# Low parts of the weights by accumulating transfers from memory, in a one-core RWKV-7 / Conformer / gated-MLP layer

## The chip, the cores and the metric

The kernel runs on one core of a Trainium2 chip. A core has five engines that run their own instruction queues in order and wait for one another through semaphores: PE (TensorE, matmuls), DVE (VectorE), ACT (ScalarE), POOL (GpSimd) and SP (SyncE, which here issues the transfers). Sixteen DMA engines move data between the device memory and the core's on-chip memory of 128 partitions. Matmuls write to PSUM, which PE, DVE and ACT reach. The metric is the time of one execution on the device in microseconds (us); lower is better.

## The reference

One layer (DEPTH = 1) on x of 1024 tokens and 1024 channels, in float32: a token mixer made of an RWKV-7 head group and a causal convolution group, then a gated MLP with a short causal convolution. All large products are with weights that come from memory.

```python
h = _rms_norm(x, norm_pre_mix[i])
p = h @ w_in                                  # (1024, 1024) x (1024, 2720)
# RWKV-7 recurrence over 8 heads of 64, causal depthwise conv of width 31, norms, gates
mix = jnp.concatenate([rwkv_out, c], axis=-1) @ w_out        # (1024, 1024) x (1024, 1024)
x = x + _rms_norm(mix, norm_post_mix[i])
h = _rms_norm(x, norm_pre_ffn[i])
hid = h @ ffn_up                              # (1024, 1024) x (1024, 5632)
hid = _causal_dwconv(hid, ffn_conv_w, ffn_conv_b)
gate, up = hid[..., :D_FF], hid[..., D_FF:]   # D_FF = 2816
f = (jax.nn.gelu(gate, approximate=True) * up) @ ffn_down    # (1024, 2816) x (2816, 1024)
x = x + _rms_norm(f, norm_post_ffn[i])
```

## The kernel before

Large products are made of three passes over PE in the type float32r. Each float32 operand is cut into a high part (the value rounded to float32r) and a low part (the value minus the high part), and the product is high x high + high x low + low x high. `split` (L145 to L148) makes the two parts: a cast by ACT, a subtraction by DVE or, with `pool=True`, by POOL.

Weights pass through `weight` (L150 to L160). Per piece of 128 x 512 elements, 256 KB, it takes a raw tile (tag `wr`, three buffers), has SP load it (L154), takes a high and a low tile (tags `wh` and `wl`, two buffers each) and calls `split` on POOL. With `held` the pair comes from another pool and is kept. `weight` is run at high priority, so that its instructions stand in each queue as early as the buffers allow. A buffer is given out again when the last reader of its former content is done; that wait, with the order of the instructions in each engine's queue, sets when a weight's cast can start. The order is fixed when the program is built: a scheduler simulates the program and places instructions by priority, stream by stream (`stream`, `PRIO`).

Who uses weights:

- `project` (called for w_in, w_wa, w_g in the mixer, and for ffn_up by `ffn_pair`): two pieces of a column block of 128 channels; per piece four k tiles x three matmuls of 512 tokens, the third of each three with the low part. The tokens go in two halves of 512, so every weight is loaded twice: 40 pieces of w_in and two each of w_wa and w_g per half, 88 of ffn_up per half.
- `w_out`: 16 pieces per half, 24 matmuls of 256 columns each.
- `ffn_down`: per half 2 x 22 pieces, each with four token tiles x three matmuls, the second with the low part. In the last column half of the last token half, the last eight pieces are `held`.

The mixer runs first (up to about 770 us in the profile), with the recurrence, convolutions and projections interleaved on PE; the first eight channel tiles of ffn_up for the first token half (32 pieces) run inside it. From there on the kernel is ffn_up and ffn_down, first for tokens 0 to 511, then for 512 to 1023. While these run, ACT evacuates each ffn_up bank (L800, `acc<-pb`), then applies gelu (L810) and rounds the result (L148, `ahi`); DVE adds the taps of the short convolution (L805).

Other work on POOL: the power -0.5 of `rstd` (L143), copies and clears, and in the recurrence the scaling of the state (L632, `XG`).

Of the kernel before, what the change touches and what calls it, by code (L numbers as in the profile page):

```python
# [13 lines left out]
F32 = mybir.dt.float32  # L14
F32R = mybir.dt.float32r
BF16 = mybir.dt.bfloat16
AF = mybir.ActivationFunctionType
ALU = mybir.AluOpType
# [73 lines left out]
class Trunk:  # L92
# [57 lines left out]
    def weight(self, src, shape, held=False):  # L150

        with self.tc.high_priority():
            raw = self.wp.tile(shape, F32, tag="wr", bufs=3, name=self.nm("wr"))
            self.nc.sync.dma_start(raw, src)  # L154
            if held:
                hi, lo = (self.hp.tile(shape, F32R, tag="h", name=self.nm("w")) for _ in range(2))
            else:
                hi, lo = (self.wp.tile(shape, F32R, tag=t, bufs=2, name=self.nm(t)) for t in ("wh", "wl"))
            self.split(hi, lo, raw, True)
        return hi, lo  # L160


# [946 lines left out]
```

## Time and profile before

| | us |
|---|---|
| runs shown, three: lowest, median, highest | 1423.25, 1438.39, 1440.5 |
| the profiled execution, its time | 1419.05 |
| the profiled execution, span from first to last instruction | 1417.2 |

The profile's numbers are those of one execution, with a mean granted TensorE clock of 0.978. Busy time is the time in which an engine ran an instruction; waits and the issuing of transfers are not in it. A row of a group gives the line, engine and operation, output <- inputs with buffer numbers left out, shape and count, then busy us and mean ns of one, then the idle time of the engine just before these instructions and what ended most of it. The chain of work that ended last is followed back from the last instruction, at each step to what released it. In the table of stretches, each engine's busy us (and instructions) stand for a piece of the span, then the granted TensorE clock as a share of full speed, the busy share of the sixteen DMA engines and the GB/s. A timeline row starts with the start and the duration in us.

### The profile page before, as it was taken

Reading aid. Unit: us, or ns where it says so; the run is one execution under the profiler, and the core shown is the slowest. Engines: PE = TensorE matmul, PEld = TensorE weight load, DVE = VectorE, ACT = ScalarE, POOL = GpSimd, SP = SyncE. Lnnn points to the kernel's source line nnn. Section 1 sums busy time; section 2 is a strip of 40 time slices with the busy share of each in tenths; the row PEclk is TensorE's granted clock in tenths of the full one; section 3 lists DMA queues with packets and bytes.
Section 4 is the critical chain, followed back from the end, with each engine's and each line's share of the span. In section 5 each row is a group of like instructions: output and inputs, shape, how many; then the busy total and the mean of one; then the engine's idle time right before and its main releaser. Section 6 shows DMA issues by size and latency. Waiting matters only on the chain.

```text
span 1417.2 us, 22810 instructions
## 1 busy us (share of the span) xinstructions
PE 1354.4 (96%) x8736; PEld 1104.2 (78%) x8736; DVE 767.6 (54%) x1346; ACT 642.4 (45%) x1275; POOL 567.6 (40%) x494
## 2 busy tenths in 40 slices
PE   6999999999987997999999999999999999999998
PEld 4777777777866896877788888888888888888886
DVE  5367798989896568874613544420015654442002
ACT  6542563466424734546534555542234444443222
POOL 3332323334421232133444554444445454444443
PEclk9999999999997998799999999999999999999999
DMA  6212211221110333222235444353334543333333
GB/s 206 82 58 66 61 38 31 67 69 60 51 43 9 103 97 103 76 66 60 80 113 187 127 126 127 97 177 91 97 97 127 154 128 98 97 97 96 91 96 112
DMA packets 71997, 133.31 MB, mean 94 GB/s; under 512 B 7760, under 2 KB 14288, under 8 KB 71888
## 3 DMA queue, kind: packets, MB, share of 16 engines
q1 hardware_dynamic: 71888, 131.85, 30.5%
q8 instruction: 69, 1.13, 0.3%
q14 instruction: 40, 0.33, 0.1%
HBM read 119.24 MB, written 12.58 MB: 93 GB/s over the span
## 4 chain that ended last, share of the span: by engine, by line
PE 86%; DVE 7%; issue 3%; ACT 2%; DMA 1%; POOL 1%; SPq 0%; DVEq 0%; POOLq 0%; ACTq 0%
PE pb L126 71%; PE pe L126 6%; PE xs L126 4%; PE Y L126 2%; PE pe L136 1%; DMA pt<-mixd 1%; DVE l L547 1%; DVE dw L520 1%; DVE pc L358 1%; PE xs L136 1%; DVE l L483 1%; DVE dw L542 0%; DMA l<-x 0%; POOL wl L148 0%; DVE sub L530 0%
## 5 line engine op out<-in xcount | busy, mean ns | idle before, releaser
L148 POOL TENSOR_TENSOR wl<-wr,wh 128x512 fp32r<-128x512 f32 x376 | 492.7, 1310 | 702.0 <-ACT wh L148 657.4
L148 ACT CAST wh<-wr 128x512 fp32r<-128x512 f32 x376 | 231.8, 616 | 506.3 <-PE pb L126 301.5
L126 PE MATMUL pb<-f,wh 128*128 128x512 f32 x1408 | 435.9, 391 | 2.4 <-ACT jk L701 1.9
L126 PEld LDWEIGHTS pb<-f,wh 128*128 128x128 f32 x1408 | 263.8, 188 | 57.1 <-ACT jk L701 2.1
L126 PE MATMUL pb<-f,wl 128*128 128x512 f32 x704 | 276.8, 393 | 2.0 <-POOL wl L148 2.0
L126 PE MATMUL pb<-h,wh 128*128 128x512 f32 (+2 forms) x704 | 230.0, 404 | 4.0 <-DVE v L298 2.0
L805 DVE SCALAR_TENSOR_TENSOR acc<-pb,params,acc 128x511 f32<-128x511 f32 (+1 forms) x144 | 107.5, 746 | 162.3 <-ACT acc L800 97.9
L358 DVE SCALAR_TENSOR_TENSOR pc<-c,params,pc 128x512 f32<-128x512 f32 x232 | 174.3, 751 | 7.3 <-ACT pc L355 2.8
L126 PEld LDWEIGHTS pb<-h,wh 128*128 128x128 f32 (+2 forms) x704 | 129.4, 187 | 37.5 <-issue 4.4
L126 PEld LDWEIGHTS pb<-f,wl 128*128 128x128 f32 x704 | 132.2, 188 | 30.3 <-POOL wl L148 2.9
L126 PE MATMUL pb<-h,wl 128*128 128x512 f32 (+2 forms) x352 | 143.9, 409 | 0.0
L126 PE MATMUL pb<-wl,ahi 128*128 128x512 f32 x320 | 126.9, 397 | 0.0
L126 PE MATMUL pb<-wh,alo 128*128 128x512 f32 x320 | 126.3, 395 | 0.0
L858 DVE TENSOR_TENSOR row<-pb,post_ffn 128x512 f32<-128x512 f32 x16 | 10.2, 685 | 209.2 <-ACT junk L857 209.2
L126 PE MATMUL pb<-wh,ahi 128*128 128x512 f32 x320 | 88.7, 397 | 0.0
L126 PEld LDWEIGHTS pb<-h,wl 128*128 128x128 f32 (+2 forms) x352 | 65.7, 187 | 19.6 <-issue 2.5
L126 PEld LDWEIGHTS pb<-wh,alo 128*128 128x128 f32 x320 | 60.1, 188 | 14.4
L126 PEld LDWEIGHTS pb<-wl,ahi 128*128 128x128 f32 x320 | 60.1, 188 | 14.3
L126 PEld LDWEIGHTS pb<-wh,ahi 128*128 128x128 f32 x320 | 59.7, 188 | 14.6
L800 ACT ACTIVATE acc<-pb,params 128x512 f32<-128x512 f32 x72 | 55.8, 775 | 0.0
L126 PE MATMUL pb<-wh,m 128*128 128x256 f32 x256 | 54.3, 304 | 0.0
L148 DVE TENSOR_TENSOR alo<-acc,ahi 128x512 fp32r<-128x512 f32 x36 | 35.0, 971 | 24.9 <-ACT ahi L148 24.9
(246 smaller groups left out, 1820.4 us busy)
## 6 DMA issues: line engine op xcount, KB each, us to landing
wr<-ffn_up SPq DMA_DIRECT2D x176, 256.0 KB, 2.6
wr<-ffn_down SPq DMA_DIRECT2D x88, 256.0 KB, 2.6
wr<-w_in SPq DMA_DIRECT2D x80, 256.0 KB, 2.6
wr<-w_out SPq DMA_DIRECT2D x32, 256.0 KB, 2.7
mixd<-t SPq DMA_DIRECT2D x16, 256.0 KB, 3.1
nrow<-x1d SPq DMA_DIRECT2D x8, 512.0 KB, 4.2
out<-nrow SPq DMA_DIRECT2D x16, 256.0 KB, 2.3
l<-x SPq DMA_DIRECT2D x8, 256.0 KB, 5.9
```

Source lines behind the costliest of these rows:

```text
L126: return self.nc.tensor.matmul(out, lhsT, rhs, start=start, stop=stop, skip_group_check=skip)
L136: self.nc.tensor.transpose(out, in_, self.con("ident")[:n, :n])
L148: return self.nc.scalar.copy(hi, src), eng.tensor_tensor(lo, src, hi.bitcast(F32), ALU.subtract)
L358: nc.vector.scalar_tensor_tensor(out, c[:, j:j + HALF], w(j), acc, ALU.mult, ALU.add)
L483: nc.vector.tensor_tensor(bv, bv, ge, ALU.mult)
L520: nc.vector.transpose(self.dw[64 * e + 32 * g:64 * e + 32 * g + 32, o:o + 512].rearrange("p (i j) -> p i j", i=16), Lq[64 + 32 * g:96 + 32 ...
L547: w.mark = nc.vector.transpose(RT[gs, :, c:c + 16].rearrange("p u i -> p i u"), self.dw[64 * e + 32 * g:64 * e + 32 * g + 32, o:o + 512].r ...
L800: nc.scalar.activation(acc, ps, AF.Identity, scale=w(2), bias=self.par("fb", ch))
L805: nc.vector.scalar_tensor_tensor(acc[:, o:], ps[:, :HALF - o], w(j), acc[:, o:], ALU.mult, ALU.add)
L858: nc.vector.tensor_tensor(f[:, cs], ps, self.post_ffn[:, cs], ALU.mult)
```

## The change

`weight` no longer calls `split`. ACT makes the high part as before, and in a second pass writes the negative of the raw tile, rounded to float32r, into the low tile. POOL then issues a transfer that loads the same weights from memory a second time and adds them to the low tile (`accum_op=ALU.add`), so that it ends as weight minus high part. The raw tile now has two buffers instead of three, the high and the low tile three instead of two. All weights go this way, the held ones too; the splits of activations stay on ACT and DVE.

```diff
     def weight(self, src, shape, held=False):
 
         with self.tc.high_priority():
-            raw = self.wp.tile(shape, F32, tag="wr", bufs=3, name=self.nm("wr"))
+            raw = self.wp.tile(shape, F32, tag="wr", bufs=2, name=self.nm("wr"))
             self.nc.sync.dma_start(raw, src)
             if held:
                 hi, lo = (self.hp.tile(shape, F32R, tag="h", name=self.nm("w")) for _ in range(2))
             else:
-                hi, lo = (self.wp.tile(shape, F32R, tag=t, bufs=2, name=self.nm(t)) for t in ("wh", "wl"))
-            self.split(hi, lo, raw, True)
+                hi, lo = (self.wp.tile(shape, F32R, tag=t, bufs=3, name=self.nm(t)) for t in ("wh", "wl"))
+
+            self.nc.scalar.copy(hi, raw)
+            self.nc.scalar.mul(lo, raw, -1.0)
+            self.nc.gpsimd.dma_start(lo, src, accum_op=ALU.add)
         return hi, lo
```

## The prediction

> **What bounds the kernel now.** First the page: busy time, the three rows of slices, the queue, the shares of the chain, and the two groups that the change is about.
>
> ```profile
> span 1417.2 us, 22810 instructions
> PE 1354.4 (96%) x8736; PEld 1104.2 (78%) x8736; DVE 767.6 (54%) x1346; ACT 642.4 (45%) x1275; POOL 567.6 (40%) x494
> ...
> q1 hardware_dynamic: 71888, 131.85, 30.5%
> ...
> PE 86%; DVE 7%; issue 3%; ACT 2%; DMA 1%; POOL 1%; SPq 0%; DVEq 0%; POOLq 0%; ACTq 0%
> ...
> L148 POOL TENSOR_TENSOR wl<-wr,wh 128x512 fp32r<-128x512 f32 x376 | 492.7, 1310 | 702.0 <-ACT wh L148 657.4
> L148 ACT CAST wh<-wr 128x512 fp32r<-128x512 f32 x376 | 231.8, 616 | 506.3 <-PE pb L126 301.5
> ```
>
> PE is busy for 96% of the span and holds 86% of the chain; POOL, whose 493 us of subtractions go, holds 1%. At most 1417.2 - 1354.4 = 63 us of PE idle time can be won. Next the stretches, to see where PE is full.
>
> ```profile
> core 0: us, PE busy (x) PEld busy (x) DVE busy (x) ACT busy (x) POOL busy (x), PEclk, DMA share, GB/s
> 0.00:420.00 420.00, 395.65 (x2988) 304.24 (x2988) 331.21 (x575) 207.42 (x403) 148.66 (x153) 0.99 0.23 70
> 0.00:768.00 768.00, 712.14 (x5920) 578.35 (x5920) 536.40 (x952) 379.30 (x797) 256.53 (x251) 0.96 0.25 75
> 420.00:440.00 20.00, 10.31 (x44) 8.22 (x44) 19.04 (x49) 6.47 (x14) 2.08 (x3) 0.67 0.00 1
> 593.00:700.00 107.00, 107.00 (x737) 85.65 (x738) 63.18 (x101) 59.30 (x125) 41.80 (x37) 1.00 0.22 67
> 718.00:768.00 50.00, 45.76 (x381) 44.55 (x379) 7.72 (x11) 17.47 (x51) 21.43 (x17) 1.00 0.44 128
> 768.00:1405.00 637.00, 636.94 (x2794) 521.86 (x2795) 226.53 (x384) 261.95 (x476) 309.98 (x242) 1.00 0.38 116
> ```
>
> From 768 to 1405 us PE is never idle: nothing can be won there, only lost. That stretch uses weights one after another, and the timeline and the chain show how.
>
> ```profile
> 902.64 0.62 ACT L148 CAST wh<-wr 128x512 fp32r<-128x512 f32 x1 [1.37 <-POOL wl L148]
> ...
> 903.34 1.38 POOL L148 TENSOR_TENSOR wl<-wr,wh 128x512 fp32r<-128x512 f32 x1 [1.42 <-ACT wh L148]
> ...
> 905.36 0.62 ACT L148 CAST wh<-wr 128x512 fp32r<-128x512 f32 x1 [1.14 <-PE pb L126]
> ...
> 905.89 0.78 ACT L800 ACTIVATE acc<-pb,params 128x512 f32<-128x512 f32 x1
> ...
> 906.06 1.29 POOL L148 TENSOR_TENSOR wl<-wr,wh 128x512 fp32r<-128x512 f32 x1 [1.34 <-ACT wh L148]
> ```
> ```profile
> 1025.38 0.62 ACT L148 CAST wh<-wr 128x512 fp32r<-128x512 f32 x1 [2.18 <-PE pb L126]
> 1028.18 0.62 ACT L148 CAST wh<-wr 128x512 fp32r<-128x512 f32 x1 [2.18 <-PE pb L126]
> ```
> ```profile
> 704.21 2.63 POOL wl L148
> ...
> 718.15 1.29 POOL wl L148
> ...
> 723.23 1.28 POOL wl L148
> ...
> 941.28 463.50 PE pb L126 x2016
> ```
>
> A weight is used by 12 matmuls: 463.50 / 2016 x 12 = 2.76 us on average, 2.72 us in ffn_up (cast to cast, 902.64 to 905.36) and 2.80 us in ffn_down (1025.38 to 1028.18). The cast starts when PE lets go of a slot, POOL follows 0.70 us later and ends 1.4 us after that, so the pair is ready about 2.1 us after the slot came free. Two slots give 2 x 2.72 - 2.72 = 2.72 us for that: 0.6 us to spare. The change has to be judged by this cycle, not by busy shares.
>
> **The change part by part.** *Slots.* Three slots instead of two: one turn may last 3 x 2.72 = 8.16 us (ffn_down 8.40). *The turn.* Cast, then the new ACT pass 0.53 us behind it (905.36 to 905.89, where ACT overlaps two passes) for 0.62 us, its price taken from the cast of the same tile; a hop of 0.70 - 0.62 = 0.08 us to POOL; the accumulating transfer, X from POOL's issue to landing; a hop of 0.08; 2.72 us of matmuls; 0.02 to the cast. That is 1.23 + 0.08 + 2.72 + 0.02 = 4.05 + X in ffn_up, 4.13 + X in ffn_down. PE stays full while X is under 4.1 us (4.27 in ffn_down); beyond that each weight costs a third of the excess.
>
> *X.* The page shows no transfer from POOL and none that adds. The nearest rows:
>
> ```profile
> wr<-ffn_up SPq DMA_DIRECT2D x176, 256.0 KB, 2.6
> ...
> nrow<-x1d SPq DMA_DIRECT2D x8, 512.0 KB, 4.2
> ...
> row<-x SPq DMA_DIRECT2D x4, 512.0 KB, 3.4
> ```
> ```profile
> DMA to landing us min/median/max: 2.0/2.6/6.9
> ```
>
> The lower end is 2.6 us (the same bytes, from SP), the upper 6.9 us (the longest landing of a weight). An adding transfer has to read the tile as well as the weight, so I price it as twice the bytes in the stage that matters: 4.2 us (nrow<-x1d). What POOL itself needs to issue it, no row shows; between 0 and 1.30 us (one of its passes over such a tile), I take the middle, 0.65. X = 4.85 us, between ends that lie far apart; nearest to the 512 KB row, because that transfer too runs beside the weight stream.
>
> The row on landing says 2.6 us for 256 KB. The Trainium skill, DMA: Bandwidth & Descriptors, section "Anatomy of one DMA — SWDGE (gpsimd) path", gives the same for a plain transfer from POOL, 2.0 us plus bytes at 436 GB/s, an estimate of 2.6 us; with twice the bytes 3.2 us, and by it the sum below would be that of the second rival. No row here shows a transfer from POOL.
>
> *ACT.* Every weight adds 0.62 us. In ffn_up the evacuation (0.78 us) becomes ready when the cast does, so the new pass can stand behind it for every second weight: 0 to 0.39 us on the mean, I take 0.2. ffn_down has ACT idle for 2.18 us before each cast: 0.
>
> *The sum, by stage.* ffn_up after 768 us, 176 - 32 = 144 weights: (4.05 + 0.2 + 4.85) / 3 = 3.03, +0.31 each, 45 us. ffn_down, 88 - 8 held = 80: 8.98 / 3 = 2.99, +0.19 each, 15 us. The held eight have buffers of their own and land ahead: 0. The 32 early ffn_up weights, 107 / 32 = 3.34 us apart: 1.33 + 0.2 + 4.85 + 3.34 = 9.72 us of 10.03: hidden behind the other PE work there, with 0.3 us to spare. The 88 projections before 420 us, 4.8 us apart, may take 14.3 us: hidden; bunched, they would pay as ffn_up does. w_out between 718 and 768 us, 16 weights of 45.76 / 16 = 2.86 us: (1.33 + 4.85 + 2.86) / 3 = 3.01 against 50 / 16 = 3.1 already taken: 2 us for unevenness. The three waits for POOL's wl on the chain (704 to 724 us) become waits for a transfer, 0.62 + 4.85 - 1.30 = 4.2 us longer each unless the third slot lets it start earlier: between 0 and 12.5, I take 6. ACT before 768 us gains 154 x 0.62 = 95 us on 379 busy; its 2% of the chain (28 us) grows by a quarter at most: 0 to 8, I take 8. Sum: 45 + 15 + 2 + 6 + 8 = 76 us.
>
> *Queues passed.* POOL: the issue waits for the ACT pass, and the rstd and recurrence work queued behind it waits too, where it waited for the cast before; 0.53 us later to start, shorter by up to 1.3 in the pass: 0, covered by POOL's 657 us of waiting for wh. SP: raw tiles go from three to two, but are free after 1.23 us instead of 2.1; 2 x 2.72 - 1.23 = 4.2 us remain for a refill that lands in 2.6: 0, and the cover is gone if landings pass 4.2. DVE: nothing.
>
> *The engines of the transfers.* q1's 30.5% of 1417.2 us is 432 us for 131.85 MB, so 0.86 us of all sixteen per 256 KB. A second stream at one to three times that makes 1.7 to 3.4 us per weight against 2.72: near the edge, a rival below.
>
> The profiled execution took 1419.05 us; the runs shown lie between 1423.25 and 1440.5, 4 to 21 us above it. 1419 + 76 + 10 = 1505 us.
>
> **The rivals.** *Forecast: the turn of three slots is too long by under a microsecond a weight.* 0.47; with X from 4.2 to 6 it gives 1440 to 1620.
>
> *The transfer is much slower, or the sixteen engines fill.* At X = 6.9 ffn_up turns in 11.15 / 3 = 3.72 (+1.00 x 144), ffn_down in 3.68 (+0.88 x 80), the early ones in 3.92 (+0.58 x 32), w_out in 3.7 (+0.6 x 16), and the 14 us of the two last terms of the sum: 144 + 70 + 19 + 10 + 14 = 257, about 1685 with the 10 us. Full engines at three times the price: 3 x 0.86 + 0.86 = 3.44 us a weight, 144 x 0.72 + 80 x 0.64 = 155 and the small terms' 16, 1600. For it: a DMA share of 0.38 already; against it: landing at 2.6 us beside that load. 0.16, at 1640.
>
> *Hidden.* X under 4.1 us: only small terms stay, 1430 (1415 to 1445). For it: 2.6 and 3.4 us for plain rows, and SP's idle queue. 0.31.
>
> *Faster.* POOL's passes over two tiles slow DVE where both run:
>
> ```profile
> L148 DVE TENSOR_TENSOR alo<-acc,ahi x36: 692/1012/1572, 785.1 to 1291.4; 128x512 fp32r<-128x512 f32 x36
> ```
>
> The same subtraction takes 0.69 us at best and 1.01 us at the median. If all DVE work on the chain (7%, 99 us) was stretched like that, 32% of it, 31 us, comes back, and with X hidden the time is 1400. It decides only if nearly all of that chain is stretched, and DVE's costly groups read PSUM. 0.04.
>
> *The clock.* Between 420 and 440 us PE was idle half the time and its granted clock was 0.67; in 718 to 768, idle 8%, it stayed 1.00. X over 12 us would idle it half the time: 5.4 us a weight, 2000 us or more. The Trainium skill, TensorE: Matmul & The Clock Gate, "Part 1: The HAM clock gate", says the clock halves after idle windows; the two rows agree. Stalls of 0.3 us per weight are far from it: 0.02.
>
> **How the numbers follow.** 1505 is that of the likeliest. The range 1418 to 1640 leaves out the fast rival and half of the slow one; the forecast alone spans 1440 to 1620. Faster or slower by over 2% is about what a measurement of this kernel can tell: below 1410, above 1467. Faster 0.05 (0.04, and 0.01 of hidden); same 0.36 (0.30 of hidden, 0.06 of the forecast with X near 4.5); slower 0.59.
>
> **What would show it.** A queue from POOL with some 96 MB more; X from its issue to landing, against 4.1 us; PE waiting for that transfer in each weight from 768 us on, PE busy there about 0.92, cast to cast near 3.0; ACT busy 642 + 384 x 0.62 = 880 us; POOL's 493 us gone. X under 4, or PE full after 768 us, makes the forecast wrong; landings of SP's weights above 4.2 us point to the engines.

## The result and the profile after

| | us |
|---|---|
| before, median of 4 runs (lowest to highest) | 1432.79 (1423.25 to 1440.5) |
| changed, median of 4 runs (lowest to highest) | 1535.69 (1529.98 to 1536.86) |
| ratio, 95% interval | 1.0714 (1.0632 to 1.0795) |
| the changed kernel's profiled execution, its time and its span | 1534.78 and 1532.9 |

The change makes the kernel 7% slower. From the page of the changed kernel, the rows that answer to those shown of before: span and busy time, the two queues, the shares of the chain, a group of matmuls that read low parts, and POOL's issues.

```profile
span 1532.9 us, 23416 instructions
...
PE 1405.5 (92%) x8736; PEld 1121.9 (73%) x8736; DVE 718.4 (47%) x1346; ACT 834.8 (54%) x1659; POOL 399.6 (26%) x494
...
q0 software_dynamic: 55296, 99.90, 40.1%
q1 hardware_dynamic: 71888, 131.85, 29.9%
...
PE 56%; DMA 21%; issue 14%; ACT 4%; DVE 2%; POOL 2%; SPq 0%; POOLq 0%; DVEq 0%; ACTq 0%
...
L126 PE MATMUL pb<-f,wl 128*128 128x512 f32 x704 | 284.3, 409 | 49.4 <-DMA wl<-ffn_up 49.1
...
L162 POOL DMA_DIRECT2D wl<-ffn_up x176 | 152.5, 866 | 436.4 <-ACT wl L161 382.7
...
wr<-ffn_up SPq DMA_DIRECT2D x176, 256.0 KB, 3.2
wl<-ffn_up POOLq DMA_DIRECT2D x176, 256.0 KB, 4.6
...
wl<-ffn_down POOLq DMA_DIRECT2D x80, 256.0 KB, 4.7
```

Transfers have taken 21% of the chain, and 14% is "issue", time for which the chain names no releaser (in the stretch below, POOL waits in it for ACT's passes); PE, which held 86%, holds 56%. The transfer that adds lands 4.6 to 4.7 us after POOL begins to issue it, and the issue itself takes POOL 0.87 us, which counts as busy time of POOL here.

PE's busy time for the same 8736 matmuls rose by 51 us, from 1354.4 to 1405.5: of the 116 us by which the span grew, 65 are idle time of PE and 51 are matmuls that took longer. In the stage after the mixer, the MLP stage, it rose by 33 us, from 640.3 to 673.4.

Where the time went, by stretches of the MLP stage (columns as before): first ffn_up, first ffn_down, second ffn_up, second ffn_down.

```profile
793.00:969.00 176.00, 159.41 (x666) 123.70 (x665) 68.34 (x102) 106.75 (x213) 49.12 (x58) 0.99 0.86 191
969.00:1110.00 141.00, 134.28 (x581) 106.13 (x581) 16.31 (x33) 67.36 (x133) 41.15 (x48) 1.00 0.91 194
1111.00:1397.00 286.00, 254.33 (x1040) 198.06 (x1039) 106.82 (x230) 150.21 (x259) 76.91 (x91) 0.96 0.82 175
1397.00:1533.00 136.00, 124.61 (x525) 97.72 (x524) 14.54 (x30) 54.19 (x102) 38.47 (x46) 0.98 0.84 177
```

In the kernel before, the first cast of an activation that opens this stage starts at 770.1 us, the first matmul of ffn_down at 922.0, the second ffn_up at 1047.5, the last low-part matmul of ffn_up at 1286.8, and the span ends at 1417.2. In the changed kernel the same events stand at 793.2, 969.3, 1106.7, 1396.8 and 1532.9. So the mixer costs 23 us, ffn_up 24 and 51, ffn_down 12 and 6: 116 us, the whole difference of the spans, and 93 of them in the MLP stage. Two thirds of it, 75 us, lie in the 144 weights of ffn_up: 0.52 us each, 3.24 us from weight to weight instead of 2.72.

The turn of a buffer can be followed there. First the chain of the changed kernel in one stretch, then the timeline rows of the same stretch.

```profile
1250.58 4.68 PE pb L126 x20
1255.26 3.01 issue
1258.29 4.52 DMA wl<-ffn_up
1262.81 0.04 issue
1262.85 4.70 PE pb L126 x20
```
```profile
1256.17 0.62 ACT L160 CAST wh<-wr 128x512 fp32r<-128x512 f32 x1 [1.56 <-PE pb L126]
1256.70 0.77 ACT L803 ACTIVATE acc<-pb,params 128x512 f32<-128x512 f32 x1
...
1257.37 0.62 ACT L161 ACTIVATE wl<-wr 128x512 fp32r<-128x512 f32 x1
...
1258.29 0.86 POOL L162 DMA_DIRECT2D wl<-ffn_up  x1 [3.02 <-ACT wl L161]
```

A matmul releases a pair; ACT casts, then evacuates a bank, and only then writes the negative; POOL issues 0.30 us after that pass has ended (1257.37 + 0.62 to 1258.29); 4.52 us later the low part is there and PE goes on. From 1250.58 to 1262.85, 12.27 us, the chain goes round once, in the time of four weights: 3.07 us each. PE waits in one of the four.

### The profile page after: what moved, and what is told of

The parts are those of the page before. It is cut to its first block, busy times and chain, and to the rows that moved or that the text cites. A ratio compares the mean times of both kernels' runs of the same rounds, so it can differ in the third digit from the quotient of the medians.

```text
span 1532.9 us, 23416 instructions
## 1 busy us (share of the span) xinstructions
PE 1405.5 (92%) x8736; PEld 1121.9 (73%) x8736; DVE 718.4 (47%) x1346; ACT 834.8 (54%) x1659; POOL 399.6 (26%) x494
## 3 DMA queue, kind: packets, MB, share of 16 engines
q0 software_dynamic: 55296, 99.90, 40.1%
## 4 chain that ended last, share of the span: by engine, by line
PE 56%; DMA 21%; issue 14%; ACT 4%; DVE 2%; POOL 2%; SPq 0%; POOLq 0%; DVEq 0%; ACTq 0%
PE pb L126 42%; DMA wl<-ffn_up 12%; PE pe L126 6%; PE xs L126 5%; PE Y L126 2%; POOL wl L162 2%; DMA wr<-ffn_down 2%; DMA wl<-w_in 2%; PE pe L136 2%; DMA wl<-w_out 1%; DMA wl<-ffn_down 1%; ACT wl L161 1%; DMA wr<-w_in 1%; PE xs L136 1%; DMA pt<-mixd 1%
## 5 line engine op out<-in xcount | busy, mean ns | idle before, releaser
L126 PE MATMUL pb<-f,wl 128*128 128x512 f32 x704 | 284.3, 409 | 49.4 <-DMA wl<-ffn_up 49.1
L161 ACT ACTIVATE wl<-wr 128x512 fp32r<-128x512 f32 x376 | 235.1, 625 | 160.1 <-PE pb L126 127.6
L126 PEld LDWEIGHTS pb<-f,wh 128*128 128x128 f32 x1408 | 269.7, 192 | 57.8 <-ACT jk L704 2.6
L162 POOL DMA_DIRECT2D wl<-ffn_up x176 | 152.5, 866 | 436.4 <-ACT wl L161 382.7
L162 POOL DMA_DIRECT2D wl<-w_in x80 | 69.6, 873 | 209.3 <-ACT wl L161 190.6
L162 POOL DMA_DIRECT2D wl<-ffn_down x80 | 69.1, 865 | 166.0 <-ACT wl L161 164.1
```

Source lines behind the costliest of these rows:

```text
L126: return self.nc.tensor.matmul(out, lhsT, rhs, start=start, stop=stop, skip_group_check=skip)
L161: self.nc.scalar.mul(lo, raw, -1.0)
L162: self.nc.gpsimd.dma_start(lo, src, accum_op=ALU.add)
```

## The experiments

Three theories were set against each other. One: the turn of the high/low pairs is too long for three slots. Two: the two raw tiles set the pace. Three: the sixteen DMA engines, 0.82 to 0.91 busy in the rows above, are full. Tests of theories one and two change buffer counts. Additional tiles come from a pool `wx` that lives from the MLP stage on; the mixer keeps the buffers of the change. Results are given as a median, with the ratio to runs of the kernel before taken beside them and its 95% interval. The medians of those runs lie between 1423 and 1430 us, so a difference between two of the runs below is known to several us only.

**A fourth pair in the MLP stage.**

```diff
         self.f2p = pool("f2p", 6)
+        self.wx = pool("wx")
...
-                hi, lo = (self.wp.tile(shape, F32R, tag=t, bufs=3, name=self.nm(t)) for t in ("wh", "wl"))
+                p, b = (self.wx, 1) if self.wx and self.nw % 4 == 3 else (self.wp, 3)
+                self.nw += bool(self.wx)
+                hi, lo = (p.tile(shape, F32R, tag=t, bufs=b, name=self.nm(t)) for t in ("wh", "wl"))
```

> The changed kernel with a fourth high/low pair of buffers from the start of the MLP stage on (after the mixer); raw tiles stay at two. Theory 1 (a turn of a high/low buffer, measured at 3 x 3.24 = 9.7 us in ffn_up, is too long for three slots): 9.7 / 4 = 2.4 us is under the 2.72 us of matmuls, so PE is full again after the mixer and the some 95 us lost there come back: 1440 us, within 15. Theory 2 (the two raw tiles set the pace: a weight's cast waits for its load): nothing changes, over 1515. Theory 3 (the sixteen DMA engines, 0.82 to 0.91 busy, are full): bytes are the same, over 1515.

Measured: 1487.59 us (1.0407; 1.036 to 1.0454). 48 us came back: more than theories two and three allow, half of what theory one asked for. The rows of ACT's waits say what came next; in the changed kernel, and then with the fourth pair:

```profile
ACT wh L160 <- DMA wr<-ffn_up: 37.4, 21, 3.3
ACT wl L161 <- DMA wr<-ffn_down: 27.0, 15, 4.0
```
```profile
ACT wh L163 <- DMA wr<-ffn_up: 126.0, 91, 4.5
...
ACT wl L164 <- DMA wr<-ffn_down: 74.1, 43, 3.5
```

With pairs to spare, ACT waits for loads of raw tiles: 126 us before casts of ffn_up weights instead of 37.

**A third raw tile alone in the MLP stage**, by the same rotation for `wr`, pairs left at three.

```diff
-            raw = self.wp.tile(shape, F32, tag="wr", bufs=2, name=self.nm("wr"))
+            p, b = (self.wx, 1) if self.wx and self.nw % 3 == 2 else (self.wp, 2)
+            self.nw += bool(self.wx)
+            raw = p.tile(shape, F32, tag="wr", bufs=b, name=self.nm("wr"))
```

> The changed kernel with a third raw tile from the start of the MLP stage on; high/low pairs stay at three. Theory 1 (the turn of the high/low buffers): the turn is the same but for casts that come late for want of a raw tile, 1505 to 1535 us. Theory 2 (the raw tiles): casts no longer wait for loads and PE is full after the mixer, 1440 to 1460. Theory 3 (full engines): 1535 as before this edit.

Measured: 1534.87 us (1.0698; 1.0593 to 1.0804): no change. Theory two falls as a first limit.

**Buffer counts as before, transfers as changed.**

```diff
-            raw = self.wp.tile(shape, F32, tag="wr", bufs=2, name=self.nm("wr"))
+            raw = self.wp.tile(shape, F32, tag="wr", bufs=3, name=self.nm("wr"))
...
-                hi, lo = (self.wp.tile(shape, F32R, tag=t, bufs=3, name=self.nm(t)) for t in ("wh", "wl"))
+                hi, lo = (self.wp.tile(shape, F32R, tag=t, bufs=2, name=self.nm(t)) for t in ("wh", "wl"))
```

> The changed kernel with the buffer counts of the kernel before: three raw tiles, two high/low pairs. Theory 1 (the turn): ffn_up 4.05 + 0.4 + 4.6 = 9.05 us over two slots, 4.5 us a weight, +1.3 on the 3.24 of the changed kernel for 144 weights; ffn_down 8.8 / 2 = 4.4, +1.4 for 80 weights: about 300 us more, 1800 to 1900, with the mixer on top. Theory 2 (the raw tiles): faster than 1535. Theory 3 (full engines): about 1535, bytes are the same.

Measured: 1941.92 us in one run, 406 us more than the changed kernel and far from the two other theories. The mixer took 67 of them (its end at 859.9 instead of 793.2 us), which theory one had not priced; the MLP stage took 341, where theory one gave about 300.

**Both: four pairs and three raw tiles in the MLP stage** (the two edits above together, with a counter each).

> Four high/low pairs and three raw tiles from the start of the MLP stage on. With four pairs alone 1487.6 us was measured, 48 of the some 95 lost after the mixer came back, and the casts there wait for loads of raw tiles (126 us of ACT's idle time before a cast). Theory 1b (after the turn of three pairs, the two raw tiles are the next limit): PE is full after the mixer, 1445 to 1460 us. Theory 3 (what is left is the sixteen DMA engines, 0.9 busy with both streams, whatever the buffers): 1480 to 1490.

Measured: 1470.58 us (1.0268; 1.0203 to 1.0332), another 17 us: the third raw tile helps once the pairs are enough. It is between the two expectations. The stretches of this kernel, first ffn_up and then the rest up to the end of the second one:

```profile
800.00:961.00 161.00, 154.42 (x662) 124.77 (x661) 68.16 (x102) 108.88 (x216) 50.83 (x60) 0.97 0.94 214
961.00:1336.00 375.00, 372.81 (x1623) 301.58 (x1622) 123.28 (x263) 219.24 (x391) 118.23 (x139) 1.00 0.95 206
```

PE is nearly full from 961 us on, and the DMA engines are 0.94 to 0.95 busy. The stretch up to 961 us still holds two long landings, and the chain shows them:

```profile
803.29 8.25 DMA wl<-ffn_up
...
860.34 6.47 DMA wl<-ffn_up
```

**No adding.** POOL's transfer writes over the tile: everything else as changed, or with four pairs and three raw tiles. The low part is then the whole weight, so these two kernels no longer compute the layer and serve for timing alone.

```diff
-            self.nc.gpsimd.dma_start(lo, src, accum_op=ALU.add)
+            self.nc.gpsimd.dma_start(lo, src)
```

> The changed kernel with POOL's transfer writing the weight instead of adding it, so that the low part is the whole weight; all waits, bytes from memory and issues stay. Theory 1: what counts is the landing. If adding is what makes it 4.6 us, it falls to 3 to 3.5 us, the turn to 8.2 to 8.6 us, 2.72 to 2.87 us a weight: 1440 to 1460. If the landing of a transfer from POOL is 4.6 us without adding too: 1535. Theory 3 (engines): their share in the MLP stage falls from 0.85 to about 0.65, and the time to 1440, with PE full even where a landing stays above 4.3 us.

> Four high/low pairs and three raw tiles in the MLP stage, and POOL's transfer writes the weight instead of adding it, so that the low part is the whole weight. With the adding transfer 1470.6 us was measured. If the rest in the MLP stage is the sixteen engines' load (a transfer that adds takes 40.1 / 24.3 = 1.65 times the share of a plain one): the MLP stage returns to its 647 us and the time to 1435 to 1450. If it is ACT's second pass and POOL's issue: 1465 to 1475.

Measured: 1452.37 us in one run with the change's buffers, 1439.38 us (1.0125; 1.0067 to 1.0183) with the larger ones. The rows of the first of them:

```profile
q0 software_dynamic: 55296, 99.90, 24.3%
...
wl<-ffn_up POOLq DMA_DIRECT2D x176, 256.0 KB, 3.3
```
```profile
L162 POOL DMA_DIRECT2D wl<-ffn_up x176: 527/527/617, 535.8 to 1310.7; - x176
```

Adding raises the landing from 3.3 to 4.6 us, the issue from 0.53 to 0.86 us, and the engines' time for the same 99.90 MB from 24.3% of 1450.6 us, 353 us, to 40.1% of 1532.9 us, 615 us: 1.74 times. Without it, three pairs are nearly enough: the MLP stage takes 675.1 us in that one run, 28 more than in the kernel before, although X (3.3 us in ffn_up, 3.9 in ffn_down) is under the 4.1 us that the prediction gave as the bound. With larger buffers 1.2% remains, of which these runs don't name the parts. With larger buffers adding costs 1470.58 - 1439.38 = 31 us (20 by the two ratios); the profiles put 7 of them in the MLP stage (669.8 us from its first cast against 662.4) and the rest before it, where profiles of the same mixer differ by up to 18.

**The place of the negative.** ACT's pass was first to go ahead of the cast in the program's order.

```diff
-            self.nc.scalar.copy(hi, raw)
             self.nc.scalar.mul(lo, raw, -1.0)
+            self.nc.scalar.copy(hi, raw)
```

> The changed kernel with the negative written ahead of the high part in the program's order, buffers as changed. Theory 1 (the turn): the transfer can start one ACT pass earlier, 0.53 us off a turn in ffn_up, where the cast goes first now; in ffn_down the negative goes first already. 0.53 / 3 x 144 = 25 us less: 1510. Rival (a turn is held by other things, the raw tile's load or ACT's evacuation between the two passes): 1525 to 1540.

Measured: 1541.98 us (1.0822; 1.0745 to 1.0898). It tells nothing of the step: the scheduler still placed the cast first in ffn_up, as the timeline shows (L161 is the cast here).

```profile
1247.32 0.62 ACT L161 CAST wh<-wr 128x512 fp32r<-128x512 f32 x1 [1.44 <-PE pb L126]
1247.84 0.78 ACT L803 ACTIVATE acc<-pb,params 128x512 f32<-128x512 f32 x1
1248.51 0.62 ACT L160 ACTIVATE wl<-wr 128x512 fp32r<-128x512 f32 x1
```

So the pass was given to DVE, with the change's buffers and with the larger ones.

```diff
-            self.nc.scalar.mul(lo, raw, -1.0)
+            self.nc.vector.tensor_scalar(lo, raw, -1.0, None, ALU.mult)
```

> The changed kernel with the negative written by DVE instead of ACT, buffers as changed. DVE has little to do in the MLP stage (busy 206 of 740 us there), so the negative can be written beside the cast and no longer stands behind ACT's evacuation. Theory 1 (the turn, with the ACT queue as the part that I priced too low): 0.53 us for the pass and 0.39 us for the evacuation leave a turn of 9.7 us in ffn_up, 0.9 / 3 x 144 = 44 us less, little in ffn_down where the negative went first already: 1490 to 1500. Rival (engines, or the load of raw tiles): over 1520. DVE has more to do in the mixer, which can give back up to 15 us.

> Four high/low pairs and three raw tiles in the MLP stage, and the negative on DVE for all weights. With buffers alone 1470.6 us was measured, 23 us of it over the kernel before in the MLP stage by the profile and the rest in the mixer. If the MLP stage's rest is ACT's queue it goes: 1445 to 1455. If it is the load of the sixteen engines: 1465 to 1475. In no case below the kernel before, whose PE is full there.

Measured: 1502.27 us (1.0552; 1.0514 to 1.0591) and 1470.07 us (1.0332; 1.0289 to 1.0376). With three pairs, 33 us come back (23 by the two ratios): from its first cast to the end, the MLP stage takes 697.5 us against 739.7, close to the 44 us that the theory asked for, and the mixer gives 10 back. With four pairs and three raw tiles it changes nothing: ACT's queue lengthened the turn, and counts only while the turn is the limit.

**Buffers and mixer apart.** The kernel before with the change's buffer counts; then the changed kernel with POOL's subtraction up to the end of the mixer, with the change's buffers and with the larger ones (`self.ffn` is set where the MLP stage's pools are made; with the larger buffers `self.wx` stands in its place).

```diff
+            if not self.ffn:
+                self.split(hi, lo, raw, True)
+                return hi, lo
             self.nc.scalar.copy(hi, raw)
```

> The kernel before with only the buffer counts of the change (two raw tiles, three high/low pairs; subtraction on POOL). Theory 1: PE was full after the mixer and stays so: within 10 us of the 1430 of the kernel before; a gain over 10 us would mean that the third pair alone is of use, a loss that two raw tiles are too few even without the second stream.

> The changed kernel with POOL's subtraction kept for all weights up to the end of the mixer (152 of 384, the early ffn_up ones among them) and the accumulating transfer only in the MLP stage. If the 23 us by which the stretch up to the MLP stage grew come from the transfers and the ACT pass there: 1535 - 23 = 1512. If they come from the buffers or from the order that the scheduler chose: 1530 to 1540.

> Four high/low pairs and three raw tiles in the MLP stage, where the accumulating transfer stays, and POOL's subtraction for all weights of the mixer, the early ffn_up ones among them. With the transfers in the mixer too, 1470.6 us was measured. If the rest is half the mixer's and half the MLP stage's, as the profiles say (the mixer some 20 us, the MLP stage 23): 1450 to 1458. If the mixer's part is not the transfers': 1465 to 1475.

Measured: 1426.92 us (0.9977; 0.9944 to 1.0009), 1525.61 us (1.0666; 1.0614 to 1.0717) and 1452.78 us (1.02; 1.0136 to 1.0264). The buffer counts alone cost nothing. Taking the transfers out of the mixer is worth 10 us with the change's buffers and 18 us with the larger ones (7 and 10 by the ratios); in the profiles the mixer then ends at 776.0 and 775.4 us, against 793.2 in the changed kernel and 770.1 before. The same mixer, in profiles of kernels that differ only in the MLP stage, ends between 781.8 and 799.6 us, so its share of the loss may be anything from 12 to 30 us.

No version was faster than the kernel before by more than the interval.

## Why the prediction was right, and where its size was off

*The bound and the direction.* PE was full after the mixer and could only lose there: 93 of the 116 us were lost there. The forecast case, a turn too long for three slots by under a microsecond a weight, is what the runs show: a slot fewer costs 406 us, one more gives 48 back. Of the signs that the prediction named, POOL's queue moved 99.90 MB (some 96 forecast), X is over 4.1 us, and PE is busy for 0.91 of the MLP stage (0.92 forecast). Two signs came otherwise. PE does not wait in each weight: it waits 59 times in that stage, 59 us in all. ACT is busy for 834.8 us and not 880, as its two passes over a tile start 0.53 us apart and take 0.62 each.

*X.* Forecast 4.85 us, measured 4.6 in ffn_up and 4.7 in ffn_down. Taking twice the bytes for a transfer that adds was close for the engines' time, 1.74 times. That the sum came so near is partly luck: POOL's issue took 0.86 us where I took 0.65, and the rest 3.7 where I took 4.2. The estimate from the Trainium skill, DMA: Bandwidth & Descriptors (section "Anatomy of one DMA — SWDGE (gpsimd) path"), 2.6 us plain and 3.2 with twice the bytes, is too low here: 3.3 and 4.6 us. By it the change would have been hidden.

*The term that was mis-sized is ffn_up: 45 us forecast, 75 measured.* The turn itself was not far off. From 1250.6 us to the end of the second ffn_up, 48 weights took 146.2 us, 3.05 each, where the forecast was 3.03. X was 4.5 us there at the median, so the rest of the turn was longer: 3 x 3.05 - 4.5 - 4.05 = 0.6 us, where the step "0 to 0.39 us on the mean, I take 0.2" stood. The evacuation did stand between the two passes (1256.70), which gives the upper end, 0.39; the hop from ACT to POOL's transfer took 0.30 us where I took 0.08. An X that was forecast too long and two steps that were forecast too short nearly cancel, which is luck. With the pass on DVE, clear of the evacuation, the MLP stage took 42 us less. With the fourth pair the weights of this piece take 2.85 us each.

Of the 30 us that are missing in the forecast, 7 lie in the first ffn_up and 23 in the first 40 weights of the second, from 1106.7 to 1250.6 us: 143.9 us, 3.60 each. The second ffn_up before the change, and then the two pieces of it in the changed kernel (columns as before):

```profile
1047.50:1286.80 239.30, 239.30 (x1057) 198.12 (x1057) 124.90 (x234) 109.76 (x180) 118.87 (x92) 1.00 0.39 115
```
```profile
1106.70:1250.60 143.90, 120.58 (x482) 95.20 (x480) 52.63 (x115) 71.39 (x127) 36.85 (x44) 0.93 0.79 177
1250.60:1396.80 146.20, 137.85 (x578) 106.42 (x578) 56.31 (x120) 82.23 (x142) 41.45 (x48) 1.00 0.84 171
```

In the first piece the transfers that add land later and less evenly, after 5.0 us at the median and 7.8 at most, against 4.5 and 5.9 in the second. The four waits of PE over 3 us in ffn_up all end with landings of 6.2 to 7.1 us. Beside three of the four, finished rows of the first 512 tokens leave for memory at that moment. First SP's rows of one such place, then the landing on the chain and the wait of PE that it ends:

```profile
1169.78 0.34 SPq L845 DMA_DIRECT2D out<-nrow  x1
1170.75 0.33 SPq L154 DMA_DIRECT2D wr<-ffn_up  x1
1171.13 0.45 SPq L845 DMA_DIRECT2D out<-nrow  x1
```
```profile
1171.70 6.58 DMA wl<-ffn_up
```
```profile
1178.33 0.79 PE L126 MATMUL pb<-f,wl 128*128 128x512 f32 x1 [3.84 <-DMA wl<-ffn_up]
```

The kernel before sends the same rows in its second ffn_up and PE is full throughout. No run takes the rows away, so it is not shown that they lengthen the landings; the first of the four long landings, at 1114.87, has none beside it. What the prediction lacked is the spread of X: it priced 4.85 us for every weight, and landings of 6 to 7 us cost PE 3 to 4 us each.

Casts that wait for a raw tile add to it:

```profile
1239.59 0.63 ACT L161 ACTIVATE wl<-wr 128x512 fp32r<-128x512 f32 x1
...
1240.24 19.70 SPq L154 DMA_DIRECT2D wr<-ffn_up  x7
...
1243.69 0.62 ACT L160 CAST wh<-wr 128x512 fp32r<-128x512 f32 x1 [2.97 <-DMA wr<-ffn_up]
```

The pass that ended at 1240.22 freed a raw tile, SP issued at 1240.24, and the cast started when the load had landed, 3.45 us later. I had 4.2 us for a refill; the landing rose from 2.6 to 3.2 us at the median, and the pass that frees the tile comes late by the evacuation. What these waits cost by themselves was not measured: a third raw tile alone changed nothing.

Longer matmuls are in the 75 us too: PE's busy time in the second ffn_up rose from 239.30 to 120.58 + 137.85 = 258.43 us, 19 of the 51 us lost there, and in the first from 151.9 to 159.5, 8 of 24. The last section shows one reason.

*ffn_down*: 15 forecast, 18 measured. There the scheduler mostly placed the negative ahead of the cast, which I had not foreseen; POOL can then start a pass earlier, more than the longer hop takes. That this is why the term came out is argued, not shown.

*The mixer*: 2 + 6 + 8 = 16 us forecast for w_out, the waits on the chain and ACT, 23 measured in the profile, with the spread told above; 7 to 18 go with the transfers. The three terms were not measured apart.

*Queues passed.* POOL's wait for ACT grew; on the chain POOL itself holds 2%, which is its issuing of transfers and part of X. SP's cover of 1.6 us shrank as said above. Two readings were off without effect on the sum: 152 and not 154 weights come before 768 us, and in the kernel before 94 of ACT's waits for a cast ended with work of POOL (128.9 us) beside 170 that ended with PE's (301.5 us).

*The rivals.* Full engines were wrong as the first limit, since the bytes are the same in the run that took 48 us off; with both buffers enlarged the engines are 0.94 to 0.95 busy and PE is nearly full beside them. Whether they are the limit of what is left there is open: without adding the MLP stage gains only 7 us more. Hidden: not with X over 4.1 us. Faster: its mechanism was there and its price was not. DVE's subtraction of activations went to its best time:

```profile
L148 DVE TENSOR_TENSOR alo<-acc,ahi x36: 691/692/695, 813.0 to 1401.4; 128x512 fp32r<-128x512 f32 x36
```

and DVE's busy time fell by 49 us, to 718, but no time came of it: in the MLP stage PE had not waited before, and the mixer grew. The clock was set aside with 0.02, since stalls of 0.3 us a weight were far from idling PE for half the time. As the sole cause it was rightly set aside: the mean granted share fell from 0.978 to 0.952. But the stalls come bunched, and behind the longest the clock did fall, so it has a share in the loss that the sum put at nothing.

*The number.* 1505 forecast, 1535.69 measured. The terms together are 40 us short, 76 against the 116 by which the spans differ: 30 in ffn_up, 3 in ffn_down, 7 in the mixer. The forecast also added 10 us, as the profiled execution before lay under the other runs; the profiled one after lies at the median of its runs, so that these 10 us made up for part of the miss, which is luck, and the numbers are 30 us apart.

## What to carry to other kernels

A chain of small steps between the release of a buffer and its next use has a budget: slots times the consumer's time. A transfer that is added to that chain has to be paid in slots (here a fourth pair and a third raw tile made PE nearly full again), and once the budget is spent every hop and every neighbour in an in-order queue is paid by the consumer at its share per slot. Write out the whole turn before pricing any step at nothing, price the spread of a landing and not only its median, and look for the second turn (here the raw tile's) that binds when the first is relaxed.

## What was not expected of the hardware

A transfer from POOL that adds took the sixteen engines 1.74 times the time of one that doesn't, for the same count of bytes in the queue's row, and POOL 0.86 instead of 0.53 us to issue. From one place of the second ffn_up on, two waits of PE, and the granted clock (the third number from the end of a row) in the stretches behind them:

```profile
1149.95 0.80 PE L126 MATMUL pb<-f,wl 128*128 128x512 f32 x1 [3.69 <-DMA wl<-ffn_up]
...
1163.27 0.51 PE L126 MATMUL pb<-f,wl 128*128 128x512 f32 x1 [0.72 <-DMA wl<-ffn_up]
```
```profile
1149.60:1153.00 3.40, 3.05 (x7) 2.50 (x8) 0.19 (x1) 0.00 (x0) 0.00 (x0) 0.50 1.07 314
1153.00:1174.40 21.40, 20.68 (x90) 16.46 (x89) 8.61 (x19) 12.23 (x22) 6.62 (x8) 1.00 0.75 166
1176.90:1183.70 6.80, 5.37 (x13) 4.22 (x14) 1.09 (x3) 1.13 (x3) 0.37 (x1) 0.50 0.76 203
```

About the end of the wait of 3.69 us the clock was at half for 3.4 us; behind the wait of 0.72 us it stayed at 1.00; with the wait of 3.84 us that ends at 1178.33 it was at half for 6.8 us. So it is in the whole MLP stage of this profile: five waits of PE took 2.7 to 3.8 us, and each brought 3.4 to 6.8 us at half the clock; the other 54, of 1.94 us and less, brought none. Stalls that are spread evenly and stalls of the same sum that come bunched are thus not the same loss. A short wait costs a little as well: the first matmul behind it took 0.51 us at 1163.27, where matmuls in an unbroken run take 0.39 to 0.40.
